# Where in their rows the streamed activation tiles begin: the B pair at 72 and the inner feed-forward pairs at 48 and 56 bytes above a multiple of 256

## The chip, the cores and the metric

The kernel runs on one core of one Trainium2 chip. The metric is the device time of one execution in microseconds (us). Of the core's engines these matter here: TensorE (PE in the profile, with its weight loads as PEld), VectorE (DVE), ScalarE (ACT), GpSimd (POOL) and SyncE (SP), which issues the transfers of the weights.

## The reference

Two decoder layers for 256 tokens of width 1024, in float32. The first has a gated delta rule and a softmax attention with forget gates side by side, and an MLP with squared ReLU; the second has a gated feed-forward, a mixer of differential and dilated attention, and a second gated feed-forward:

```python
u = rmsnorm(x, norm_mix_g);  proj = u @ w_in                # 9 kinds of columns
y_a = gated_delta_rule(...) @ w_proj_gdn;  y_b = forgetting_attention(...) @ w_proj_fox
h = x + (sigmoid(gate_a) * y_a + sigmoid(gate_b) * y_b) @ w_out
x = h + square(relu(rmsnorm(h) @ w_up)) @ w_down            # 1024 -> 4096 -> 1024
x = x + 0.5 * (silu(n(x) @ w_gate) * (n(x) @ w_up)) @ w_down    # 1024 -> 2816 -> 1024
x = x + token_mixer(n(x)) @ w_out
x = x + 0.5 * (silu(n(x) @ w_gate2) * (n(x) @ w_up2)) @ w_down2
return n(x)
```

Most of the work is products of a [256, k] activation with weights that are read from memory once.

## The kernel before

Activations stand transposed: 128 of the features on the partitions, then the feature block k, then the 256 tokens, so that one block of one tile is a row of 256 float32 values, 1,024 bytes, on each partition. To keep float32 accuracy with the faster float32r matmuls, every activation and every weight is held as a pair, a rounded high part and the rest as a low part (`h` and `l`, `hi` and `lo`). One product of a 128 x 128 block of weights with a row is then three matmuls: high weights with the high row (line 258), high weights with the low row (line 259), low weights with the high row (line 260). The weights are the stationary side, the row of 256 values is the moving side.

`Feed` brings the weights in: one transfer of 1 MB for two units, then for each unit of 128 x 1024 a cast to the high part on ScalarE (line 220) and a subtraction to the low part on VectorE (line 221). The split tiles `wh` and `wl` go round in five buffers each. `gemm_tile` runs over the feature blocks of one output tile and takes the next unit when it needs one; one unit is eight blocks, 24 matmuls.

The order is written out by hand: a main line of generators yields after each few matmuls, and side lines (attention heads, norms, the delta rule) put in their small instructions when an estimated clock of the main line reaches them. No program decides it by durations at run time.

The streamed activations are in a few pairs of tiles, held by tile pools that lay tiles one behind the other on each partition:

- `Ah`, `Al` (A) and `Bh`, `Bl` (B), from the pool `xp`, made by `xpair` and used in turn by the stages. A feeds the input projections of the first layer, the projection of the delta rule, its MLP's first product and the mixer's projections. B feeds the projection of the forgetting attention, `w_out`, and the first product (gate and up) of both feed-forwards. `load_bias` puts two tables into B's place while the mixer runs.
- `ah`, `al`: the inner activations, 32 blocks in the MLP (in `first_block`) and 22 in each feed-forward (`swiglu`). They feed the second product.
- `oa2h`, `oa2l`, `ob2h`, `ob2l`: the mixer's results, four blocks each.

`operand` allocates such a tile with `off` unused float32 values ahead of it, and returns the rows behind them; in this kernel every `off` is 0. The function is called by `xpair`, which looks the offset up in `PLACE` by the tile's name, and by `first_block` and `swiglu` for `ah` and `al`.

The small matmuls that come between the long loops are those of the norm's column sums (line 449: four with one moving column each), of its row of scales (line 468: four), and the transposes for the output (line 516).

Of the kernel before, what the change touches and what calls it, by code (L numbers as in the profile page):

```python
# [9 lines left out]
F32R = mybir.dt.float32r  # L10
# [5 lines left out]
P = 128  # L16
T = 256
# [95 lines left out]
def nm(g, s):  # L113
    g.n += 1
    return f"{s}_{g.n}"
# [10 lines left out]
@contextmanager  # L126
def side_banks(g):

    with g.tc.tile_pool(name=nm(g, "psw"), bufs=4, space=bass.MemoryType.PSUM) as g.psw:
        yield  # L130
# [37 lines left out]
def scale_rows(g, out, src, col):  # L168

    g.nc.scalar.activation(out=out, in_=src, func=AF.Identity, scale=col)  # L170


def split_act(g, hi, lo, src):

    g.nc.scalar.copy(hi, src)
    g.nc.vector.tensor_tensor(out=lo, in0=src, in1=hi.bitcast(F32), op=ALU.subtract)
# [59 lines left out]

MM = 0.114

PLACE = {}


def operand(pool, nk, off, tag, name):

    t = pool.tile([P, off + nk * T], F32R, tag=tag, name=name)
    return t[:, off:].rearrange("p (k t) -> p k t", t=T)
# [20 lines left out]
def gemm_pair(g, x, nk):  # L266
    ps = gbank(g).rearrange("p (j t) -> p j t", j=2)
    for j in range(2):
        yield from gemm_tile(g, ps[:, j], x, nk)
    return ps  # L270
# [44 lines left out]
def gemm_nat(g, x):  # L315
    return (yield from gemm_nats(g, x, 1))[0]
# [43 lines left out]
def xpair(g, slot):  # L360

    return tuple(operand(g.xp, KT, PLACE.get(slot + p, 0), slot + p, nm(g, slot + p)) for p in "hl")


def gemm_add(g, src, nk, x, scale, nxt):

    for m in range(0, KT, 2):
        if m == 0 and nk == KT:
            ps = yield from gemm_first(g, src, nk)
            for j in range(2):  # L370
                add_tiles(g, x, ps[j].unsqueeze(1), j, 1, scale, None)
            nxt.pair(0)
        elif m + 2 < KT:
            ps = yield from gemm_pair(g, src, nk)
            add_tiles(g, x, ps, m, 2, scale, nxt)
        else:
            for j in (m, m + 1):
                ps = gbank(g)[:, :T].unsqueeze(1)
                yield from gemm_tile(g, ps[:, 0], src, nk)
                add_tiles(g, x, ps, j, 1, scale, nxt)  # L380
# [640 lines left out]
def first_block(g, x, a):  # L1021
# [10 lines left out]
    with ExitStack() as c1:  # L1032
        act = c1.enter_context(tc.tile_pool(name="b1act", bufs=1))
# [120 lines left out]
    with ExitStack() as c1:  # L1154
        c1.enter_context(side_banks(g))
        act = c1.enter_context(tc.tile_pool(name="mlp", bufs=1))
        tmp = c1.enter_context(tc.tile_pool(name="mlpt", bufs=2))
        nf = F1 // P
        ah = operand(act, nf, 0, "ah", "ah")
        al = operand(act, nf, 0, "al", "al")  # L1160
        late = Late(g, ln.spawn(hn.scales(), 1.5), 1)

        def relu2(m, ps):
            r = tmp.tile([P, 2, T], F32, tag="r", name=nm(g, "r"))
            nc.vector.scalar_tensor_tensor(out=r, in0=ps, scalar=0.0, in1=hn.row2, op0=ALU.max, op1=ALU.mult)
            nc.scalar.activation(out=r, in_=r, func=AF.Square)
            split_act(g, ah[:, m : m + 2], al[:, m : m + 2], r)

        for m in range(0, nf, 2):
            ps = yield from gemm_pair(g, hn.x, KT)  # L1170
            late(lambda m=m, ps=ps: relu2(m, ps))
        nxt = Norm(g, x, g.par["ffn1"], "B")
        yield from gemm_add(g, (ah, al), nf, x, 1.0, nxt)
# [6 lines left out]
def swiglu(g, x, u, after, out=None):  # L1180
    nc, tc, ln = g.nc, g.tc, g.lines
    nf = F2 // P
    with ExitStack() as c1:
        c1.enter_context(side_banks(g))
        act = c1.enter_context(tc.tile_pool(name=nm(g, "ffn"), bufs=1))
        tmp = c1.enter_context(tc.tile_pool(name=nm(g, "ffnt"), bufs=2))
        ah = operand(act, nf, 0, "ah", nm(g, "ah"))
        al = operand(act, nf, 0, "al", nm(g, "al"))
        late = Late(g, ln.spawn(u.scales(), 1.5), 1)
        gated = {}  # L1190

        def gate(m, pg):
            s = gated[m] = tmp.tile([P, 2, T], F32, tag="s", name=nm(g, "s"))
            nc.vector.tensor_tensor(out=s, in0=pg, in1=u.row2, op=ALU.mult)
            nc.scalar.activation(out=s, in_=s, func=AF.Silu)  # L1195
            nc.gpsimd.tensor_tensor(out=s, in0=s, in1=u.row2, op=ALU.mult)  # L1196

        def up(m, pu):
            s = gated.pop(m)
            nc.vector.tensor_tensor(out=s, in0=pu, in1=s, op=ALU.mult)  # L1200
            split_act(g, ah[:, m : m + 2], al[:, m : m + 2], s)

        for m in range(0, nf, 2):
            for f in (gate, up):
                ps = yield from gemm_pair(g, u.x, KT)
                late(lambda f=f, m=m, ps=ps: f(m, ps))
        if after:
            nxt = Norm(g, x, *after)
        else:
            nxt = Final(g, x, g.par["final"])  # L1210
        yield from gemm_add(g, (ah, al), nf, x, 0.5, nxt)
        if not after:
            ln.finish(*ln.sides)
            nxt.write(out)
    return nxt
# [109 lines left out]
def mixer(g, x, u, bias, gain, slot):  # L1325
    nc, tc, ln = g.nc, g.tc, g.lines
    with ExitStack() as c1:
        c1.enter_context(side_banks(g))
        act = c1.enter_context(tc.tile_pool(name="mixa", bufs=1))
        g.deep = 8  # L1330
        tmp = g.mx = c1.enter_context(tc.tile_pool(name="mixt", bufs=2))

        lam = g.small.tile([P, 4], F32, tag="lam", name="lam")
        lp = g.par["lam"].rearrange("p (i n) -> p i n", i=4)
        lt = tmp.tile([P, 2, 64], F32, tag="lt", name="lt", bufs=1)
        nc.vector.tensor_tensor(out=lt[:, 0], in0=lp[:, 0], in1=lp[:, 1], op=ALU.mult)
        nc.vector.tensor_tensor(out=lt[:, 1], in0=lp[:, 2], in1=lp[:, 3], op=ALU.mult)
        nc.vector.tensor_reduce(out=lam[:, 0:2], in_=lt, axis=AX.X, op=ALU.add)
        nc.scalar.activation(out=lam[:, 0:2], in_=lam[:, 0:2], func=AF.Exp)
        nc.vector.tensor_tensor(out=lam[:, 2:3], in0=lam[:, 0:1], in1=lam[:, 1:2], op=ALU.subtract)  # L1340
        nc.vector.tensor_scalar(
            out=lam[:, 3:4], in0=lam[:, 2:3], scalar1=LAM0, scalar2=-1.0, op0=ALU.add, op1=ALU.mult
        )
        late = Late(g, ln.spawn(u.scales(), 1.5), 1)
        have = {}

        def transposed(name, scale):
            t = act.tile([P, 4, T], F32, tag=name, name=name)

            def scaled(m, ps):  # L1350
                nc.vector.scalar_tensor_tensor(
                    out=t[:, m : m + 2], in0=ps, scalar=scale, in1=u.row2, op0=ALU.mult, op1=ALU.mult
                )

            for m in range(0, 4, 2):
                ps = yield from gemm_pair(g, u.x, KT)
                late(lambda m=m, ps=ps: scaled(m, ps))
            return t

        def natural(name):  # L1360
            t = act.tile([P, 2, 512], F32, tag=name, name=name)
            ps = yield from gemm_nat(g, u.x)
            for i in range(2):
                scale_rows(g, t[:, i], ps[i], u.col[:, i : i + 1])
            have[name] = t

        oa = [act.tile([P, 4, T], F32R, tag="oa" + p, name="oa2" + p) for p in "hl"]
        ob = [act.tile([P, 4, T], F32R, tag="ob" + p, name="ob2" + p) for p in "hl"]
        qa = yield from transposed("qa", 0.125)
        ka = yield from transposed("ka", 1.0)  # L1370

        def two(f, *rest):
            for i in rest[0]:
                yield from f(g, i, *rest[1:])

        diff = [ln.spawn(diff_head(g, i, qa, ka, bias, lam[:, 3:4], have, oa)) for i in range(4)]
        yield from natural("va")
        qb = yield from transposed("qb", 0.125)
        kb = yield from transposed("kb", 1.0)
        dil = [ln.spawn(dilated_pair(g, j, qb, kb, bias, have, ob)) for j in range(4)]  # L1380
        yield from natural("vb")

        def project(src, ks, nu, last=None):
            return project_part(g, src, ks, nu, lambda m, ps: add_tiles(g, x, ps, m, 2, 1.0, last))

        ln.finish(*diff)
        yield from project(oa, (0, 1, 2, 3), 2)
        ln.finish(*dil)
        nxt = Norm(g, x, gain, slot)
        yield from project(ob, (0, 1, 2, 3), 2, nxt)  # L1390
    return nxt
# [225 lines left out]
```

## Time and profile before

| | |
|---|---|
| median of three runs | 1060.54 us (1059.9 to 1066.08) |
| the profiled execution, its own time | 1059.77 us |
| span of its trace | 1058.0 us |
| mean granted TensorE clock | 0.975 |
| TensorE busy | 1006.4 us, 95% |
| VectorE, ScalarE busy | 695.6 us, 66%; 558.9 us, 53% |
| read from memory | 178 MB, 171 GB/s over the span |

A busy TensorE says little by itself, since matmuls overlap in it: a record lasts about 280 ns, while the next one starts some 115 ns later. How fast it goes is seen in the distance between starts. In the stages the order of time is: the first layer's projections until 388 us (the granted clock is at half for 48 us between 295 and 357 us, where TensorE has little to do), its MLP's first product to 479 us and second to 570 us, the first feed-forward's two products to 695 and 757 us, the mixer to 865 us, and the second feed-forward's two products to 986 and 1049 us.

### The profile page before, as it was taken

The numbers are of one execution on the slowest core, as the hardware profiler recorded it, in microseconds if no ns is written. First come the engines' busy times: TensorE is split into PE (matmuls) and PEld (weight loads), VectorE is DVE, ScalarE is ACT, GpSimd is POOL, SyncE is SP. The second block draws the span as 40 slices with busy tenths as digits, with TensorE's granted clock in tenths as the row PEclk, the third lists the DMA queues.
The fourth block names the chain that finished last, engine by engine and source line by source line (L and its number), as shares of the span: only waits on it lengthen the run. The fifth ranks groups of instructions, "written<-read, shape, count | busy, mean of one in ns | idle before, by whom it ended". The sixth has DMA issues, their size and how long they took to land.

```text
span 1058.0 us, 20140 instructions
## 1 busy us (share of the span) xinstructions
PE 1006.4 (95%) x8126; PEld 976.3 (92%) x8126; DVE 695.6 (66%) x1194; ACT 558.9 (53%) x1000; POOL 204.9 (19%) x379
## 2 busy tenths in 40 slices
PE   8999999999907799999999999999999999999997
PEld 7888999999907799999999999999989899999997
DVE  6676887975773587665555665676775677666553
ACT  6766765645512356654444544435566755444443
POOL 1367250002430320000000111140104511121000
PEclk9999999999957899999999999999999999999999
DMA  8645356554430145555545545457653445554451
GB/s 288 243 176 200 123 187 190 203 169 144 141 97 6 55 185 199 200 181 180 198 174 186 199 171 189 163 192 231 223 189 135 148 157 200 200 199 162 165 179 53
DMA packets 47373, 181.93 MB, mean 172 GB/s; under 512 B 20128, under 2 KB 22576, under 8 KB 29488
## 3 DMA queue, kind: packets, MB, share of 16 engines
q1 hardware_dynamic: 45888, 175.38, 47.9%
q0 software_dynamic: 960, 4.74, 1.3%
q8 instruction: 63, 1.03, 0.4%
q10 hardware_dynamic: 432, 0.53, 0.1%
q14 instruction: 30, 0.25, 0.1%
HBM read 178.25 MB, written 2.38 MB: 171 GB/s over the span
## 4 chain that ended last, share of the span: by engine, by line
PE 65%; DVE 4%; POOL 2%; DMA 1%; ACT 1%; issue 1%; SPq 0%; DVEq 0%; ACTq 0%; POOLq 0%
PE g L259 19%; PE g L258 19%; PE g L260 19%; DVE wl L221 1%; PE g L349 1%; PE g L350 1%; PE g L351 1%; DVE sol L707 1%; DVE stmp L703 1%; PE g L310 1%; PE g L308 1%; PE g L309 1%; PE w L1226 1%; POOL rsq L153 0%; PE w L949 0%
## 5 line engine op out<-in xcount | busy, mean ns | idle before, releaser
L221 DVE TENSOR_TENSOR wl<-raw,wh 128x1024 fp32r<-128x1024 f32 (+2 forms) x347 | 418.6, 1210 | 207.8 <-ACT wh L220 200.8
L220 ACT CAST wh<-raw 128x1024 fp32r<-128x1024 f32 (+2 forms) x347 | 343.7, 995 | 339.0 <-PE g L259 296.4
L260 PE MATMUL g<-Bh,wl 128*128 128x256 f32 x816 | 227.6, 280 | 0.0
L259 PE MATMUL g<-Bl,wh 128*128 128x256 f32 x816 | 227.5, 279 | 0.0
L258 PE MATMUL g<-Bh,wh 128*128 128x256 f32 x816 | 227.0, 279 | 0.0
L260 PE MATMUL g<-Ah,wl 128*128 128x256 f32 x776 | 218.0, 281 | 0.0
L259 PE MATMUL g<-Al,wh 128*128 128x256 f32 x776 | 217.9, 281 | 0.0
L258 PE MATMUL g<-Ah,wh 128*128 128x256 f32 x776 | 217.4, 281 | 0.3 <-DVE fnat L981 0.3
L260 PE MATMUL g<-ah,wl 128*128 128x256 f32 x608 | 170.1, 280 | 1.2 <-DVE wl L221 1.2
L258 PE MATMUL g<-ah,wh 128*128 128x256 f32 x608 | 170.3, 280 | 0.0
L259 PE MATMUL g<-al,wh 128*128 128x256 f32 x608 | 170.2, 280 | 0.0
L258 PEld LDWEIGHTS g<-Bh,wh 128*128 128x128 f32 x816 | 154.4, 190 | 0.1
L259 PEld LDWEIGHTS g<-Bl,wh 128*128 128x128 f32 x816 | 153.2, 188 | 0.2
L260 PEld LDWEIGHTS g<-Bh,wl 128*128 128x128 f32 x816 | 153.2, 188 | 0.1
L260 PEld LDWEIGHTS g<-Ah,wl 128*128 128x128 f32 x776 | 147.1, 190 | 0.1
L258 PEld LDWEIGHTS g<-Ah,wh 128*128 128x128 f32 x776 | 145.7, 188 | 0.8 <-DVE fnat L981 0.7
L259 PEld LDWEIGHTS g<-Al,wh 128*128 128x128 f32 x776 | 145.9, 188 | 0.3 <-DVE Al L411 0.2
L260 PEld LDWEIGHTS g<-ah,wl 128*128 128x128 f32 x608 | 115.5, 190 | 1.4 <-DVE wl L221 1.4
L258 PEld LDWEIGHTS g<-ah,wh 128*128 128x128 f32 x608 | 114.3, 188 | 0.0
L259 PEld LDWEIGHTS g<-al,wh 128*128 128x128 f32 x608 | 114.3, 188 | 0.0
L1196 POOL TENSOR_TENSOR s<-s,row 128x512 f32<-128x512 f32 x22 | 37.7, 1715 | 207.7 <-ACT s L1195 207.7
L427 POOL TENSOR_TENSOR acc<-acc,sq 128x512 f32<-128x512 f32 x10 | 14.1, 1413 | 244.5 <-ACT sq L422 244.5
(321 smaller groups left out, 1387.3 us busy)
## 6 DMA issues: line engine op xcount, KB each, us to landing
raw<-in_w_in_dram SPq DMA_DIRECT2D x44, 1024.0 KB, 4.8
raw<-in_ffn_gu_dram SPq DMA_DIRECT2D x44, 1024.0 KB, 4.7
raw<-in_ffn_dn_dram SPq DMA_DIRECT2D x32, 704.0 KB, 4.0
raw<-in_w_up_dram SPq DMA_DIRECT2D x16, 1024.0 KB, 4.8
raw<-in_w_down_dram SPq DMA_DIRECT2D x16, 1024.0 KB, 4.8
raw<-in_w_out_dram SPq DMA_DIRECT2D x8, 1024.0 KB, 4.8
raw<-in_w_proj_fox_dram SPq DMA_DIRECT2D x4, 1024.0 KB, 4.9
raw<-in_w_proj_gdn_dram SPq DMA_DIRECT2D x4, 1024.0 KB, 4.8
```

Source lines behind the costliest of these rows:

```text
L220: nc.scalar.copy(hi[:, r], raw[:, r])
L221: nc.vector.tensor_tensor(out=lo[:, r], in0=raw[:, r], in1=hi.bitcast(F32)[:, r], op=ALU.subtract)
L258: nc.tensor.matmul(out, lhsT=w_h, rhs=xh[:, k, :], start=(k == 0), stop=False)
L259: nc.tensor.matmul(out, lhsT=w_h, rhs=xl[:, k, :], start=False, stop=False)
L260: nc.tensor.matmul(out, lhsT=w_l, rhs=xh[:, k, :], start=False, stop=(k == nk - 1))
L308: nc.tensor.matmul(ps[b][t], lhsT=a_h, rhs=w_h, start=(k == 0), stop=False)
L309: nc.tensor.matmul(ps[b][t], lhsT=a_l, rhs=w_h, start=False, stop=False)
L310: nc.tensor.matmul(ps[b][t], lhsT=a_h, rhs=w_l, start=False, stop=(k == KT - 1))
L349: nc.tensor.matmul(ps[:, j], lhsT=hi[:, c], rhs=src[0][:, k], start=(i == 0), stop=False)
L350: nc.tensor.matmul(ps[:, j], lhsT=hi[:, c], rhs=src[1][:, k], start=False, stop=False)
L427: e.tensor_tensor(out=acc, in0=acc, in1=sq, op=ALU.add)
L1196: nc.gpsimd.tensor_tensor(out=s, in0=s, in1=u.row2, op=ALU.mult)
```

## The change

Tiles begin elsewhere in their partitions; the values, the instructions, their order on each of the five engines and the waits stay what they were. In the built program before, all streamed pairs (A, B, `ah`/`al`, `oa`, `ob`) begin 64 bytes above a multiple of 256, and all ten weight tiles 128 bytes above. As a block is 1,024 bytes, every row of a tile has the same remainder. With the change both tiles of B begin at 72, `ah` and `al` of the MLP at 48, those of the feed-forwards at 56. A, `oa`, `ob` and the weights keep theirs; the offset of 56 values for `oa2h` is there because the tiles ahead of it have moved by 32. The offsets differ between the tiles of a pair for the same reason. The bias tables in B's place move by 32 bytes in one of two cases, and so do the small tiles of the attention and of the delta rule, which lie behind.

```diff
-PLACE = {}
+PLACE = {"Bh": 2, "Bl": 58}
...
         nf = F1 // P
-        ah = operand(act, nf, 0, "ah", "ah")
-        al = operand(act, nf, 0, "al", "al")
+        ah = operand(act, nf, 52, "ah", "ah")
+        al = operand(act, nf, 60, "al", "al")
...
-        ah = operand(act, nf, 0, "ah", nm(g, "ah"))
-        al = operand(act, nf, 0, "al", nm(g, "al"))
+        ah = operand(act, nf, 54, "ah", nm(g, "ah"))
+        al = operand(act, nf, 62, "al", nm(g, "al"))
...
-        oa = [act.tile([P, 4, T], F32R, tag="oa" + p, name="oa2" + p) for p in "hl"]
+        oa = [operand(act, 4, 56 if p == "h" else 0, "oa" + p, "oa2" + p) for p in "hl"]
```

## Rows read from the trace of the kernel before

**Rows 1.** The page's parts 1 and 2: busy time, and the granted clock in 40 slices.

```profile
span 1058.0 us, 20140 instructions
...
PE 1006.4 (95%) x8126; PEld 976.3 (92%) x8126; DVE 695.6 (66%) x1194; ACT 558.9 (53%) x1000; POOL 204.9 (19%) x379
...
PEclk9999999999957899999999999999999999999999
```

**Rows 2.** The page's part 4: the chain that ended last, shares by engine and line.

```profile
PE 65%; DVE 4%; POOL 2%; DMA 1%; ACT 1%; issue 1%; SPq 0%; DVEq 0%; ACTq 0%; POOLq 0%
PE g L259 19%; PE g L258 19%; PE g L260 19%; DVE wl L221 1%; PE g L349 1%; PE g L350 1%; PE g L351 1%; DVE sol L707 1%; DVE stmp L703 1%; PE g L310 1%; PE g L308 1%; PE g L309 1%; PE w L1226 1%; POOL rsq L153 0%; PE w L949 0%
```

**Rows 3.** TensorE's waits over the run: line, waited for, total us, times, longest.

```profile
PE g L260 <- DVE wl L221: 1.2, 1, 1.2
```

**Rows 4.** Groups by line, 479.2 to 569.7 us: count | busy us, mean ns | idle.

```profile
L258 PE MATMUL g<-ah,wh 128*128 128x256 f32 x256 | 72.0, 281 | 0.0
```

**Rows 5.** Timeline of TensorE: start us, us, instruction; four starts that bound two stretches.

```profile
479.31 0.28 PE L258 MATMUL g<-ah,wh 128*128 128x256 f32 x1
...
569.76 0.28 PE L258 MATMUL g<-Bh,wh 128*128 128x256 f32 x1
...
881.91 0.28 PE L258 MATMUL g<-Bh,wh 128*128 128x256 f32 x1
...
986.29 0.28 PE L258 MATMUL g<-ah,wh 128*128 128x256 f32 x1
```

**Rows 6.** Groups by line again, 881.9 to 986.25 us.

```profile
L258 PE MATMUL g<-Bh,wh 128*128 128x256 f32 x307 | 84.8, 276 | 0.0
```

**Rows 7.** Windows, line 258 alone: stretch, us, PE busy (count) PEld busy (count), clock, DMA.

```profile
394.40:479.20 84.80, 66.97 (x238) 44.77 (x239) 1.00 0.53 188
569.80:694.95 125.15, 98.59 (x352) 67.21 (x353) 1.00 0.50 175
695.00:711.90 16.90, 12.65 (x45) 8.55 (x45) 1.00 0.67 251
763.20:815.70 52.50, 26.44 (x94) 17.64 (x94) 1.00 0.46 161
872.30:881.80 9.50, 6.88 (x25) 4.55 (x25) 1.00 0.60 212
1006.20:1045.60 39.40, 30.75 (x109) 20.29 (x109) 1.00 0.39 129
```

**Rows 8.** Timeline of TensorE around 712 us, with the idle time before.

```profile
712.12 0.38 PE L260 MATMUL g<-ah,wl 128*128 128x256 f32 x1 [1.16 <-DVE wl L221]
...
712.70 0.28 PE L258 MATMUL g<-ah,wh 128*128 128x256 f32 x1
...
713.04 0.28 PE L258 MATMUL g<-ah,wh 128*128 128x256 f32 x1
```

**Rows 9.** Timeline of TensorE around 872 and 881 us (the last window ends early).

```profile
871.71 0.50 PE L449 MATMUL w<-ones,acc 128*128 128x1 f32 x4
...
872.51 0.28 PE L258 MATMUL g<-Bh,wh 128*128 128x256 f32 x1
...
872.86 0.28 PE L258 MATMUL g<-Bh,wh 128*128 128x256 f32 x1
...
881.23 0.61 PE L468 MATMUL w<-con,col 128*128 128x128 f32 x4
...
881.23 0.27 PE L468 MATMUL w<-con,col 128*128 128x128 f32 x1
```

**Rows 10.** The page's costliest groups and the groups by form: count | busy us, mean ns.

```profile
L221 DVE TENSOR_TENSOR wl<-raw,wh 128x1024 fp32r<-128x1024 f32 (+2 forms) x347 | 418.6, 1210 | 207.8 <-ACT wh L220 200.8
...
L258 PE MATMUL g<-Bh,wh 128*128 128x256 f32 x816 | 227.0, 279 | 0.0
...
L258 PE MATMUL g<-ah,wh 128*128 128x256 f32 x608 | 170.3, 280 | 0.0
...
L176 DVE TENSOR_TENSOR al<-s,ah 128x512 fp32r<-128x512 f32 x22 | 15.0, 684 | 0.0
```

## The prediction

> **What bounds the kernel now.** I read the page's busy shares first, then the chain that ended last, TensorE's waits, and last the spacing of the matmuls themselves. TensorE is busy 95% of the span, VectorE 66% [rows 1]. Two thirds of the chain are its own instructions, with lines 258, 259 and 260 at 19% each and nothing else above 1% [rows 2]. Those are the three matmuls of `gemm_tile`. They wait for almost nothing: 1.2 us for `wl` in the whole run is the largest [rows 3]. So there the time is a count of matmuls times their spacing, and only the spacing can be won or lost.
>
> The reader should look at that spacing. In the MLP's second product 768 matmuls (256 on each line [rows 4]) start between 479.31 and 569.76 us [rows 5]: 90.45 / 768 = 117.8 ns each. In the last gate/up product, 921 (307 on line 258 [rows 6], and three lines) start between 881.91 and 986.29 us [rows 5]: 104.38 / 921 = 113.3 ns each. [...] I call these the long and the short step; the difference is 4.44 ns. The mean of one record tells them apart too: 281 ns in one and 276 ns in the other [rows 4, 6].
>
> The step belongs neither to an operand nor to a stage. `ah` has the long step from 695 to 711.9 us (12.65 us over 45 records is 281 ns [rows 7]), and after a wait of 1.16 us for `wl` the same loop goes on with 0.34 us from one matmul of line 258 to the next, three steps of 113 ns [rows 8]. `Bh` has 0.35 us for three, 117 ns, behind four small matmuls of line 449 [rows 9], and 113 ns behind four of line 468 [rows 5, 9]. Between such breaks a step is kept for hundreds of matmuls. That looks like two streams that keep a phase: the moving rows of one matmul and the weights loaded for the next, read from the same memory. A break sets the phase anew. This is my reading; the rows show only the two levels and where they change.
>
> **The change part by part.** No instruction is added, removed or moved, no wait changes, and no transfer changes in size. What moves is where the moving rows begin: until now all streamed pairs begin 64 bytes above a multiple of 256 and all weight tiles 128 above. Afterwards A and oa/ob stay at 64, B is at 72, the MLP's inner pair at 48 and both feed-forwards' at 56.
>
> Count of what is touched: B 816 x 3 = 2448 and `ah`/`al` 608 x 3 = 1824, together 4272 matmuls [rows 10]. Nothing in this trace has these distances, so I bound the price of one. From above in gain: TensorE's bare rhythm with a weight load per matmul and a short moving side. Line 468's four take 0.61 us where one takes 0.27 [rows 9], so they are (0.61 - 0.27) / 3 = 0.11 us apart; I read 110 ns, give or take one. From the other side: the long step, and one more step of 4.44 ns above it. Between these ends I take the short step. It is the lower of the two that this very operation shows, and a long step at 64/128 is a relation of two addresses and a phase which the change breaks.
>
> The sum: touched matmuls at the long step now are, counting line 258 and taking three lines, 256 in the MLP's second product, 352 in the first gate/up, 45 before 711.9 us, 25 in 872 to 882 us and 109 in 1006 to 1046 us [rows 4, 7]: 787 x 3 = 2361. At 4.44 ns that is **10.5 us**. A's matmuls keep their address, but the phase with which they begin comes out of the stages ahead of them. Their long stretches hold 238 + 94 on line 258 [rows 7], 332 x 3 = 996 matmuls, or 4.4 us. I take half, **2.2 us**, as the rows show both steps after breaks [rows 8, 9].
>
> Taken at nothing: the writes of the moved tiles. One `al` write is 684 ns on VectorE [rows 10]; it lies under a product of tens of us. If each took twice as long, only the last one before each of seven hand-overs to a moved tile would show, 7 x 0.7 = 4.9 us. The weights' split has room as well: 1,210 ns per unit on VectorE [rows 10] stand against 24 x 113 = 2,720 ns of matmuls. The small tiles that move by 32 bytes along with them feed matmuls outside the three lines; I take nothing.
>
> The profiled execution took 1059.8 us (span 1058.0), 0.8 below the median of 1060.5. 1059.8 - 10.5 - 2.2 = 1047.
>
> [...]
>
> **The rivals.** *Nothing systematic.* The steps depend on the phase alone, and moving tiles only draws the breaks again. For it: all addresses are alike now and both steps occur. Against it: one address relation cannot show whether another would be freer. Time: between one large stretch more and one less; the first gate/up alone is 352 x 3 x 4.44 = 4.7 us, so 1055 to 1065, at 1060.
>
> *A still shorter step.* Without the meeting of the two streams the spacing would fall to the bare rhythm. For it: line 468 does run there [rows 9]. Against it: the streamed ones are never seen below 113. It takes another 2.3 to 4.3 ns from each touched matmul, 10 to 18 us: 1059.8 - 10.5 less that is 1031 to 1039. [...]
>
> *Odd starts cost* (the other side). If rows that begin 8 bytes off disturb the stream, the touched matmuls that now have the short step, 4272 - 2361 = 1911, go to the long one: 1911 x 4.44 = 8.5 us, 1068. If it also adds a further step to all of them, 4272 x 4.44 = 19 us more, 1087. It decides as soon as more touched matmuls gain a step than lose one. For it: the present starts are round and the new ones are not. Against it: nothing in the rows. [...]
>
> **How the numbers follow.** Short step kept in touched stages (1043 to 1053): 0.42. Still shorter (1031 to 1039): 0.17. Nothing systematic (1055 to 1065): 0.24. Odd starts cost (1063 to 1087): 0.17. The prediction is 1047. The range 1034 to 1068 leaves out half of the shorter-step case and half of the costly one. About 1%, 10.6 us, is what a measurement of this kernel can tell from none, so the marks are 1050 and 1071. Faster: all of the shorter step, three quarters of the likeliest and a little of the third, 0.17 + 0.31 + 0.03 = 0.51. Slower: two thirds of the costly case, 0.11. The rest, 0.38, is within 1%.
>
> **What would show it.** Same counts on every line, same order. From 479 to 570 us and in the first gate/up, the matmuls of lines 258 to 260 should be 113.3 ns apart with 276 ns records, also behind the small matmuls of lines 449 and 468 and past the transposes of line 516. A's stages may show either step. I am wrong if touched stages show the long step over hundreds of matmuls, or a spacing that is neither of the two, or if A's step worsens by as much as the others gain. The granted clock should stay at 1.00 there, and waits for `wl` should stay near 1 us: at a shorter step the splits are due sooner.

## The result and the profile after

The changed kernel took 1075.26 us (median of four, 1074.83 to 1075.87) against 1061.03 us for the kernel before: 1.0125 times as long, with a 95% interval from 1.0092 to 1.0158. The prediction was 1047 us with 1034 to 1068 as its range. The time lies above the range and the sign is wrong.

The page of the changed kernel, parts 1, 2 and 5 (the groups are line, engine, operation, tiles, count | busy us, mean ns | idle before):

```profile
span 1073.1 us, 20141 instructions
...
PE 1024.1 (95%) x8126; PEld 994.7 (93%) x8126; DVE 693.9 (65%) x1194; ACT 559.6 (52%) x1000; POOL 205.1 (19%) x379
...
PEclk9999999999957899999999999999999999999998
...
L259 PE MATMUL g<-Bl,wh 128*128 128x256 f32 x816 | 233.2, 286 | 0.0
L258 PE MATMUL g<-Bh,wh 128*128 128x256 f32 x816 | 230.3, 283 | 0.0
L260 PE MATMUL g<-Bh,wl 128*128 128x256 f32 x816 | 229.2, 281 | 0.0
...
L258 PE MATMUL g<-ah,wh 128*128 128x256 f32 x608 | 171.7, 282 | 0.0
```

Beside [rows 1] and [rows 10] only TensorE differs by more than 2 us: the counts are the same, the granted clock is down in the same slices (and a tenth lower in the last one), and VectorE is 1.7 us less busy. One record of B is now 281 to 286 ns, where 276 and 281 were the two values before [rows 4, 6].

TensorE's longest waits hold none of the streamed loops; the 1.2 us for `wl` of [rows 3] is gone:

```profile
PE w L839 <- ACT tt L170: 28.5, 2, 27.8
PE w L919 <- ACT tt L170: 8.0, 2, 6.9
PE g L1443 <- POOL ones L1438: 1.0, 1, 1.0
PE g L308 <- ACT wh L220: 0.9, 1, 0.9
```

So the loss must be in the spacing. These are the first matmuls of five stages in the timeline of the changed kernel (start us, us, instruction):

```profile
480.45 0.28 PE L258 MATMUL g<-ah,wh 128*128 128x256 f32 x1
...
572.03 0.28 PE L258 MATMUL g<-Bh,wh 128*128 128x256 f32 x1
...
699.68 0.28 PE L258 MATMUL g<-ah,wh 128*128 128x256 f32 x1
...
871.71 0.28 PE L258 MATMUL g<-Bh,wh 128*128 128x256 f32 x1
...
999.34 0.28 PE L258 MATMUL g<-ah,wh 128*128 128x256 f32 x1
```

In the MLP's second product the same 768 matmuls take 572.03 - 480.45 = 91.58 us, 119.2 ns each, instead of 117.8 [rows 5]. From one stage's start to the next the two timelines give:

| stage (moved tile) | begins at | before, us | after, us | difference |
|---|---|---|---|---|
| attention's projection and `w_out` (B) | 72 | 32.47 + 22.60 | 32.81 + 23.71 | +1.4 |
| MLP, second product (`ah`) | 48 | 90.45 | 91.58 | +1.1 |
| first gate/up (B) | 72 | 125.26 | 127.65 | +2.4 |
| first feed-forward, second product (`ah`) | 56 | 61.88 | 63.54 | +1.7 |
| second gate/up (B) | 72 | 120.93 | 127.63 | +6.7 |
| second feed-forward, second product (`ah`) | 56 | 62.87 | 64.89 | +2.0 |
| MLP, first product (A, not moved) | 64 | 91.39 | 91.34 | 0.0 |
| mixer (A, `oa`, `ob`, not moved) | 64 | 108.46 | 108.49 | 0.0 |

The moved stages lose 15.3 us. What is not in the table changes by -0.3 us in all: -0.7 ahead of the first layer's input projections, +0.8 in these (A, not moved) and -0.4 between the attention's projection and `w_out`. The span grew by 15.1 us. The stage that lost most is the one that had the short step before.

Within B's loop the timeline of the changed kernel shows one pattern for hundreds of matmuls:

```profile
650.00 0.28 PE L258 MATMUL g<-Bh,wh 128*128 128x256 f32 x1
650.12 0.29 PE L259 MATMUL g<-Bl,wh 128*128 128x256 f32 x1
650.25 0.28 PE L260 MATMUL g<-Bh,wl 128*128 128x256 f32 x1
...
650.73 0.28 PE L258 MATMUL g<-Bh,wh 128*128 128x256 f32 x1
```

Six matmuls in 0.73 us, rounded; over the stretch the three take 360 ns, 120.0 ns each. That is neither the short step of 113.3 nor the long one of 117.8, and it is the same behind line 449, behind line 468 and in both gate/up products. A third level goes with the new start.

### The profile page after: what moved, and what is told of

It reads as the page before. It is cut to its first block, busy times and chain, and to the rows that moved or that the text cites. A ratio compares the mean times of both kernels' runs of the same rounds, so it can differ in the third digit from the quotient of the medians.

```text
span 1073.1 us, 20141 instructions
## 1 busy us (share of the span) xinstructions
PE 1024.1 (95%) x8126; PEld 994.7 (93%) x8126; DVE 693.9 (65%) x1194; ACT 559.6 (52%) x1000; POOL 205.1 (19%) x379
## 4 chain that ended last, share of the span: by engine, by line
PE 66%; DVE 3%; POOL 3%; ACT 1%; issue 1%; DMA 0%; DVEq 0%; SPq 0%; ACTq 0%; POOLq 0%
PE g L259 19%; PE g L260 19%; PE g L258 19%; PE g L349 1%; PE g L350 1%; PE g L351 1%; PE g L310 1%; PE g L308 1%; DVE sol L707 1%; PE g L309 1%; DVE stmp L703 1%; POOL rsq L153 1%; PE w L1226 1%; POOL rsq L152 1%; DVE wl L221 0%
## 5 line engine op out<-in xcount | busy, mean ns | idle before, releaser
L259 PE MATMUL g<-Bl,wh 128*128 128x256 f32 x816 | 233.2, 286 | 0.0
L258 PE MATMUL g<-Bh,wh 128*128 128x256 f32 x816 | 230.3, 283 | 0.0
L259 PEld LDWEIGHTS g<-Bl,wh 128*128 128x128 f32 x816 | 156.4, 192 | 0.1
```

What stands on the lines that cost most here:

```text
L258: nc.tensor.matmul(out, lhsT=w_h, rhs=xh[:, k, :], start=(k == 0), stop=False)
L259: nc.tensor.matmul(out, lhsT=w_h, rhs=xl[:, k, :], start=False, stop=False)
```

## The experiments

In all experiments but the changed kernel itself, `operand` gives each tile of a streamed pair 256 bytes of room, so that the row can begin at any remainder while its neighbours keep theirs. A table names the remainder (above a multiple of 256 bytes) for each stage: A0 and A1 are A's first two uses in the first layer, A2 and A3 are A in the MLP's first product and in the mixer, B0 and B1 are B in the attention's projection and in `w_out`, B2 and B3 in the first and second gate/up, M, F1 and F2 the inner pairs of the MLP and of the two feed-forwards. What is not named begins at 64; the weights begin at 128. The three matmuls stand on lines 259 to 261 there, the small ones on lines 451, 470 and 518. In these tables, as printed here, one number stands for both rows of a pair. A time without an interval is one execution, beside one of the kernel before on the same chip.

```diff
-def operand(pool, nk, off, tag, name):
+def operand(pool, nk, where, tag, name):
-    t = pool.tile([P, off + nk * T], F32R, tag=tag, name=name)
-    return t[:, off:].rearrange("p (k t) -> p k t", t=T)
+    off = (PLACE.get(where, (64, 64))["hl".index(tag[-1])] - 64) % 256 // 4
+    t = pool.tile([P, 64 + nk * T], F32R, tag=tag, name=name)
+    return t[:, off : off + nk * T].rearrange("p (k t) -> p k t", t=T)
```

I call the step of a stage the median, over its stretch, of the mean of six neighbouring distances between starts, taken from the trace's start times in ns. At some starts the single distances run through a fixed cycle, and the step is its middle: at 68 in sweep_c (below) a group of three lines takes 363, 369, 367 and 361 ns in turn, over the whole stretch.

**Theory.** The distance between where the moving row begins and where the weights begin, modulo 256, sets the step; some distances hold one step, others two. **Rivals.** The phase alone (new addresses only draw the two old steps again); odd starts (a row that begins off a multiple of 16 costs something); the moved neighbours or the room.

**The room alone (pad_64).**

> All streamed pairs get 256 bytes of room and keep 64 above a multiple of 256, weights at 128. Every theory: the two steps of the kernel before, 113.3 and 117.8 ns, in the long stretches and nothing above; time 1050 to 1070 us. If a long stretch shows 119 to 120 ns here, the room or the shifted bases cost it and not the remainder.

It took 1063.1 us beside 1063.8 us for the kernel before. Steps: 117.8 in the MLP's first and second product and the first gate/up, both steps in the other stages, nothing above, as before. The first gate/up, grouped by line:

```profile
L259 PE MATMUL g<-Bh,wh 128*128 128x256 f32 x281 | 79.0, 281 | 0.0
```

Room and shifted bases show no cost. The low tiles of the pairs lie another 256 bytes on here, modulo 512, and the steps are the same.

**Two sweeps (sweep_a, sweep_b).**

```diff
+PLACE = {"A2": 0, "M": 32, "B2": 96, "F1": 128, "A3": 160, "B3": 192, "F2": 224}    # sweep_a
+PLACE = {"A2": 16, "M": 80, "B2": 112, "F1": 144, "A3": 176, "B3": 208, "F2": 240}  # sweep_b
```

> Same room; the MLP's first product begins at 0, its second at 32, the first feed-forward's products at 96 and 128, the mixer's projections at 160, the last feed-forward's products at 192 and 224. Theory of the address relation: each stage has a step of its own that holds in all its long stretches, and at least one of them is neither 113.3 nor 117.8 ns. Rival, the phase alone: only 113.3 and 117.8 ns, mixed as the breaks draw them. Rival, odd starts: all of these are multiples of 16 (and of 32), so no stage above 117.8 ns.

> As sweep_a with 16, 80, 112, 144, 176, 208 and 240. Address relation: steps that differ from stage to stage; whether 48 of the changed kernel (119.2 ns) has neighbours alike at 16 and 80 shows if odd multiples of 16 cost by themselves. Phase alone: only 113.3 and 117.8 ns. Odd starts by 16: none above 117.8 ns.

| begins at | 0 | 16 | 32 | 48 | 64 | 80 | 96 | 112 |
|---|---|---|---|---|---|---|---|---|
| step, ns | 118.8, some 120.0 | 118.7, some 116.7 | 117.3 | 119.3 | 113.3 or 117.8 | 119.3 | 118.3 | 117.3 |

| begins at | 128 | 144 | 160 | 176 | 192 | 208 | 224 | 240 |
|---|---|---|---|---|---|---|---|---|
| step, ns | 120.0 | 116.7, some 113.3 | 117.7, some 116.7 | 118.3 | 117.8 | 120.0 | 120.0 | 113.3 |

(48 is from the changed kernel, 64 from the kernel before.) Where two steps stand, they change at a break. At 32 and 80 the only stretch measured is the MLP's second product, which has no break: these starts were drawn once here. The first group is 128 in sweep_a (first feed-forward, second product), the second 208 in sweep_b (second gate/up):

```profile
L259 PE MATMUL g<-ah,wh 128*128 128x256 f32 x172 | 48.7, 283 | 0.0
```

```profile
L260 PE MATMUL g<-Bl,wh 128*128 128x256 f32 x308 | 86.9, 282 | 0.0
L261 PE MATMUL g<-Bh,wl 128*128 128x256 f32 x308 | 86.8, 282 | 0.0
```

The records of 282 and 283 ns go with 120.0 ns, as in the changed kernel. Both rivals fall: there are more than two steps, and 128, 208 and 224 are multiples of 16 and have 120.0 ns, as 72 has. With 1070.8 and 1068.6 us both kernels were slower than the one before (1063.8).

**B alone (only_b72).**

```diff
+PLACE = {"B0": 72, "B1": 72, "B2": 72, "B3": 72}
```

> Only B begins at 72; the inner pairs stay at 64. Address relation: B's long stretches at 120 ns as in the changed kernel, the inner pairs' back at 113.3 or 117.8 ns; B's 2448 matmuls cost some 8 to 11 us over the kernel before, the rest of the 15 us is gone. Phase alone: B's stretches could be at 113 or 118 ns again.

1071.8 us. B had 120.0 ns in all stages, the inner pairs 113.3 and 117.8 again. The MLP's second product:

```profile
L259 PE MATMUL g<-ah,wh 128*128 128x256 f32 x253 | 71.1, 281 | 0.0
```

**Move the weights instead (weights_160).**

```diff
+    pool("skip", 1).tile([P, 8], F32, tag="skip", name="skip")
     g.hl = pool("hl", 5)
...
+PLACE = {"A2": 64, "M": 96, "B2": 160, "F1": 16, "A3": 96, "B3": 96, "F2": 64}   # the rest 96
```

> All ten weight tiles begin 32 bytes later, at 160. The MLP's first product, its second, the first feed-forward's two, the mixer's projections and the last feed-forward's two begin at 64, 96, 160, 16, 96, 96 and 64. If the distance to the weights decides, each stage repeats the step of the remainder 32 lower in the runs with weights at 128: 117.3 (as 32), 113.3 or 117.8 (as 64), 120.0 (as 128), 113.3 (as 240), 113.3 or 117.8, 113.3 or 117.8, 117.3 ns. If the moving row's own remainder decides, whatever the weights do: 113.3 or 117.8 (64), 118.3 (96), 117.7 (160), 118.5 (16), 118.3, 118.3, 113.3 or 117.8 ns.

Measured: 118.7, 113.3, 120.0, 113.3, 117.7 (with some 113.3), 113.3 (with some 117.8) and 118.3 ns. The MLP's second product at 96 and the first gate/up at 160:

```profile
L259 PE MATMUL g<-ah,wh 128*128 128x256 f32 x256 | 70.7, 276 | 0.0
```

```profile
L259 PE MATMUL g<-Bh,wh 128*128 128x256 f32 x306 | 86.6, 283 | 0.0
```

This run decides between the row's own start and the distance. 96 had 118.3 ns with weights at 128 and has 113.3 with weights at 160; 160 had 117.7 and now has 120.0, the step of 128 with weights at 128; 16 had 118.7 and now has 113.3, the step of 240. In five stages of seven the distance foretells the step. The other two, at 64, have medians of 118.7 and 118.3, where the distance gave 117.3 and the row's own remainder 113.3 or 117.8.

The trace shows how they miss. These are the second feed-forward's second product up to the first transposes of line 518, and a stretch between two such breaks:

```profile
985.78 0.28 PE L259 MATMUL g<-ah,wh 128*128 128x256 f32 x1
...
1005.49 0.28 PE L259 MATMUL g<-ah,wh 128*128 128x256 f32 x1
1005.61 0.38 PE L518 MATMUL w<-con,xg 128*128 128x128 f32 x2
...
1006.64 0.28 PE L259 MATMUL g<-ah,wh 128*128 128x256 f32 x1
...
1021.60 0.28 PE L259 MATMUL g<-ah,wh 128*128 128x256 f32 x1
```

The first stretch has 168 distances: (1005.49 - 985.78) / 168 = 117.3 ns, as foretold, and its groups of three lines go through the cycle of the row at 32 in sweep_a (350, 353, 350, 352 and 355 ns in turn). Behind the break it is (1021.60 - 1006.64) / 126 = 118.7 ns, the step that the MLP's first product keeps behind its own breaks. So this distance holds two steps, as 64 does with weights at 128, and the sweep had drawn one of them. In these runs the distance decides which steps can occur, and where there are two, a break chooses.

**A good distance everywhere (all_240, all_240_timed).**

```diff
+PLACE = {"A0": 240, "A1": 240, "A2": 240, "A3": 240, "B0": 240, "B1": 240, "B2": 240, "B3": 240, "M": 240, "F1": 240, "F2": 240}
```

> A, B and the inner pairs all at 240, weights at 128. If 240 has the short step as its own, as the last feed-forward's second product had in sweep_b (440 of 514 at 113.3 ns): 113.3 ns in all long stretches, also behind lines 449 and 468, and 1045 to 1050 us. If 240 has two steps as 64 has, and sweep_b met the better one: some long stretches above 117 ns, 1055 to 1065 us.

> The same kernel as all_240, timed. If its single time of 1047 us was the kernel's: 1046 to 1050 us, 1.0 to 1.4% under the kernel before. If it was one fortunate execution: some runs above 1055 us.

The first run took 1047.4 us; timed, the median was 1048.06 us (1046.15 to 1049.63) beside 1060.73, 0.9879 of the kernel before with an interval from 0.9854 to 0.9904. It is faster than the kernel before by 1.2%, and the changed kernel was slower than that one. The timed kernel's page, parts 1 and 5:

```profile
span 1046.4 us, 20141 instructions
...
PE 996.5 (95%) x8126; PEld 965.4 (92%) x8126; DVE 695.2 (66%) x1194; ACT 559.5 (53%) x1000; POOL 207.1 (20%) x379
...
L260 PE MATMUL g<-Bl,wh 128*128 128x256 f32 x816 | 224.8, 276 | 0.0
L259 PE MATMUL g<-Bh,wh 128*128 128x256 f32 x816 | 224.4, 276 | 0.0
...
L261 PE MATMUL g<-ah,wl 128*128 128x256 f32 x608 | 167.4, 275 | 0.8 <-DVE wl L221 0.8
```

And its timeline where the MLP's second product begins and ends:

```profile
478.05 0.28 PE L259 MATMUL g<-ah,wh 128*128 128x256 f32 x1
...
565.09 0.28 PE L259 MATMUL g<-Bh,wh 128*128 128x256 f32 x1
```

(565.09 - 478.05) / 768 = 113.3 ns, where [rows 5] give 117.8. The means of 275 and 276 ns hold for all of B and the inner pairs, so the short step returned behind each break, also behind lines 451 and 470. The one wait for `wl` is 0.8 us: the faster loop is not starved.

**Fine steps (sweep_c).**

```diff
+PLACE = {"A2": 60, "M": 68, "B2": 248, "F1": 244, "A3": 236, "B3": 232, "F2": 252}
```

> Fine steps: the seven stages begin at 60, 68, 248, 244, 236, 232 and 252. If the relation is one of whole 16 or 64 byte pieces, 4 bytes to either side of 64 or 240 cost at once (119 to 120 ns), as 72 and 56 did. If it is a matter of time (4 bytes are one column), the neighbours lie between: 114 to 118 ns.

1081.0 us, the slowest of all. 118.8 at 60, 121.7 at 68, 121.2 at 248, 121.8 at 244, 120.0 at 236 and 232, 117.8 or 120.0, by the break, at 252. The MLP's second product at 68:

```profile
L259 PE MATMUL g<-ah,wh 128*128 128x256 f32 x253 | 72.2, 285 | 0.0
L260 PE MATMUL g<-al,wh 128*128 128x256 f32 x252 | 71.9, 285 | 0.0
```

One column to either side of the good starts loses all of the gain and more. The levels do not lie in between.

**The parts, timed (only_b72_timed, only_inner).**

```diff
+PLACE = {"M": 48, "F1": 56, "F2": 56}   # only_inner
```

> Only B at 72, timed. Address relation: the stretches of only_b72 again, B at 120.0 ns, 1070 to 1073 us, two thirds or more of the change's loss.

> B stays at 64, the inner pairs go to 48 and 56 as in the change. Address relation: 119.3 ns in the MLP's second product, 120.0 in the feed-forwards', B at 113.3 or 117.8; with 1.1, 1.6 and 2.1 us over the kernel before in these three stages, 1065 to 1067 us. If the loss were the moved neighbours or the writes and not the row's start: B's stages slower too, or the loss not in these stages.

B alone: 1073.46 us, 1.0121 (1.0102 to 1.0139), 0.5 above what was expected. The inner pairs alone: 1067.23 us, 1.0064 (1.0043 to 1.0085), 0.2 above; their steps were 119.3, 120.0 and 120.0, B's 117.8 and 113.3. Both parts are slower by themselves. Together they would give 1.9%, and the change gave 1.25%. One reason is in the traces: in the timed trace of B alone the first feed-forward's second product, at 64, ran with the long step throughout, 762.86 - 699.39 = 63.47 us, 1.6 us more than in the kernel before; in the earlier trace of the same kernel it had mostly the short step. With the inner pairs at 56 this stage takes 63.54 us, so the same 1.6 us stand in both parts. Other stages at 64 drew the long step too: beside the kernel before, the second feed-forward's second product took 0.7 us more in the trace of B alone, and `w_out` 0.7 us more in that of the inner pairs. There the first feed-forward's second product also kept a wait for `wl` of 1.1 us, which the changed kernel has not.

**Steps put on other stages (swapped).**

```diff
+PLACE = {"A2": 240, "M": 72, "B2": 48, "F1": (240, 72), "A3": 64, "B3": 56, "F2": (72, 240)}   # (high, low)
```

> The remainders change stages: 240 in the MLP's first product, 72 in its second, 48 and 56 in the first products of the feed-forwards, and in the feed-forwards' second products one row of the pair at 240 and the other at 72. If the step goes with the remainder: 113.3, 120.0, 119.3, 120.0 ns, and between 113 and 120 where the rows differ. If it goes with the stage or its breaks: the steps of the changed kernel, 117.8, 119.3, 120.0, 120.0 ns.

Measured: 113.3, 120.0, 119.3 and 120.0 in A2, M, B2 and B3, all as the remainder says. A3, at 64, had 117.7 with some 113.3. With two different rows the step was 118.8 at (240, 72) and 120.7 at (72, 240); the latter does not lie between 113 and 120, as had been expected. The MLP's second product at 72:

```profile
L260 PE MATMUL g<-al,wh 128*128 128x256 f32 x256 | 73.2, 286 | 0.0
L259 PE MATMUL g<-ah,wh 128*128 128x256 f32 x256 | 72.3, 283 | 0.0
L261 PE MATMUL g<-ah,wl 128*128 128x256 f32 x255 | 71.4, 280 | 0.0
```

The pattern of B at 72 in the changed kernel, 286, 283 and 281 ns, has come over to `ah` with the start, to a nanosecond. The step belongs to the start and not to the tile or the stage; breaks only choose where a start holds two.

## Why the prediction was wrong

*What bounds the kernel.* Right. The counts, the order and the clock stayed (1.00 in the long stretches of both traces), the waits too but for the 1.2 us for `wl`, and the 15 us are distances between matmuls.

*Two steps, changed at breaks.* Right: neither of the two long stretches with 117.8 and 113.3 ns has idle time [rows 4, 6], and 0, 16, 144, 160 and 252 also show two steps that change at breaks. The trace of one kernel at one distance could not show that the short step is rare: of the 25 remainders measured with weights at 128 only 64, 144 and 240 ever showed 113.3 ns.

*"Between these ends I take the short step."* This is the step that failed. It rested on the idea that a break with the old relation frees the streams from meeting, and the experiments show that 17 of the 24 other remainders are worse than even the long step, among them all three of the change: 119.3 ns at 48 and 120.0 at 56 and 72. The term was -10.5 us and measured +15.3. By the prediction's own count: 2361 matmuls at 117.8 and 1911 at 113.3 are 115.8 ns in the mean; 768 at 119.3 and 3504 at 120.0 are 119.9; 4.1 ns on 4272 matmuls are 17.5 us. The lost wait of 1.2 us for `wl` goes off; the last us lies in the attention's projection, where the side lines' matmuls stand between the touched ones: the count gives 192 x 6.7 ns = 1.3 us, and the stage took 0.3 longer. The bound itself, one step above the long one (122.2 ns), did hold the truth, and with no row at any other distance the middle between its ends of 110 and 122 ns, 116 ns and so no gain, had as much for it as the short step. The other end, 110 ns, was misread: line 468 multiplies plain float32 tiles (`con`, `col`), not float32r. With 256 moving columns such matmuls have longer records in the trace of the kernel before, 379 ns where the streamed ones have 276 and 281 [rows 4, 6], so line 468 sets no bound for the streamed ones:

```profile
L761 PE MATMUL w<-kq 128*128 128x256 f32 x32 | 7.9, 379 | 0.0
```

*A's half, 2.2 us.* Wrong: the two stretches that it counted, the MLP's first product and the mixer, took the same time to 0.1 us, and the first of them had the long step almost throughout in both kernels. The input projections, also on A, took 0.8 us more.

*What was taken at nothing.* Right as far as the runs show: in only_b72 and only_inner the neighbours keep their remainders and the loss is there, and in the changed kernel no wait for a write or a split came onto the path.

*The rivals.* "Odd starts cost" had the sign and the time (1068 to 1087, measured 1075) and got a chance of 0.17. Its mechanism was not the cause: 128, 208 and 224 cost 120.0 ns too. No run shows a term that gives the low end of its range, 1063 us; with 119.3 ns at 48 and 120.0 at 56 and 72 the moved stages lost 15.3 us. "Nothing systematic" and "a still shorter step" fell; nothing below 113.3 ns was seen in any run's long stretches.

*What stays open.* That the distance decides which steps occur is shown by weights_160 and swapped, for weights at 128 and 160. Why it does is not. What other engines access at the time plays no part that shows: between 600 and 690 us of the changed kernel all 249 groups of three lines without a break took 360 ns, while VectorE was busy 60% of the time and ScalarE 46%. That two reads of one memory meet, the moving row's and the weights', is only my reading: no run shows the meeting itself, nor why some distances hold two steps and 240 only one.

## What to carry to other kernels

When matmuls follow each other without waits, measure the distance between their starts by stage and compare it with the other stages of the same shape: two levels there are worth as much as a wait (here 90.45 us at 64 and 87.04 us at 240 for the MLP's second product). Where the operand's start against the weights' start sets the level, one run can give each stage its own start and so try seven at once; take the start that holds its good level behind every break. A stage without a break has shown one draw only: 32 looked like 117.3 ns alone until weights_160 drew the other step of its distance, 118.7 ns. Before such a sweep, a new start is a draw among levels most of which are worse than the best one seen (here 22 of 25 remainders never showed 113.3 ns), and the forecast should say so.

## What the runs showed of the hardware that I had not expected

A float32r matmul with 256 moving columns and a weight load of its own had 113.3 ns at best and 121.8 ns at worst, at mean granted clocks of 0.975 and 0.976 over these runs (all_240_timed, sweep_c), by where the row begins against the weights alone. 4 bytes were enough: 113.3 ns at 240, 121.8 at 244 (sweep_c). The trace's start times show fixed cycles behind several of these steps, such as 363, 369, 367 and 361 ns for three matmuls at 68. At 64 the step also differed between two executions of one kernel, on two chips: the first feed-forward's second product had mostly 113.3 ns in the first trace of B alone and 117.8 ns throughout in the second.
